# Splitting four weight tiles early in a one-core decoder-layer kernel, and loading them as ready-made parts

## The chip, the cores and the metric

The kernel runs on 1 core of one Trainium2 chip. The metric is the device time of one launch in microseconds (us), as a median of several runs; one further execution was taken by the hardware profiler, and all rows below are of that execution.

## The reference, cut to what matters

One layer of a decoder is computed for 1024 prompt positions and 64 sample positions (8 sequences of 8), model width 1024, all in float32.

```python
h = rmsnorm(x, norm_mix)
q, k, v, gu, gv, ga, gb = split_in(h @ w_in)
o = attention over a window of 128 with sinks (q, k, v)        # prompt; samples with a cache
s = spatial_gating(gelu(gu), layernorm(gelu(gv)))              # gMLP branch
merged = sigmoid(ga) * (o @ w_pa) + sigmoid(gb) * (s @ w_pb)   # w_pa: 1024 x 1024, w_pb: 768 x 1024
x = x + merged @ w_out
x = x + conv_ffn(rmsnorm(x, norm_ffn))
y = rmsnorm(x, norm_final)
```

The change concerns `w_pa`, the weight of the attention branch: eight tiles of 128 output columns each, and only how four of them reach on-chip memory.

## The kernel before, in words

**Precision.** Each float32 operand of a large matmul is split in two parts of the type that TensorE takes at its faster rate: `hi` is a rounded copy, `lo = x - hi`. A product is then three matmuls, hi·hi, hi·lo and lo·hi. The helper `split` (lines 39 to 41) makes the copy on ScalarE (ACT, line 40) and the difference on VectorE (DVE, line 41).

**Weights.** The class `Weights` streams all weight tiles in a fixed order of units. A tile is loaded raw by SyncE's DMA queue (SP) into one of four `wraw` buffers (line 146), split into one of four `wh`/`wl` slots in two halves of 128x512, and handed to the matmuls by `get()`. In its ordinary use `get()` splits one unit ahead and loads three ahead. There is also a form `add_pre`: the parts lie ready in device memory, and the unit is two DMAs straight into `wh` and `wl`, with no raw buffer and no split (line 194). Before the change only the first up-projection pairs (`upd`) go that way.

**Stages around the change.** All tokens are in two groups: group 0 has the 64 sample tokens and 512 prompt tokens (576 columns), group 1 the other 512 prompt tokens.
1. The pair phase (to about 454 us): the input projection as 17 pairs of tiles, each by a seven-product scheme (`Chain.product`, line 301). After each product `behind(at, j)` takes one job from a list: first `done` and `jobs`, then `lns` (layer norm and gMLP mixing, `mix_job`), then two steps of `prep` (the loads of `prepare_samples`). The last pairs are number 14 and 15, both over both groups (15 runs group 0's seven products, then group 1's), and number 16, over group 1 alone.
2. Attention of group 0 (about 454 to 572 us), interleaved with the matmuls of the gMLP branch (`branch`, line 241, tile `s`): eight tiles of `w_pb`.
3. The opening of group 1's attention (about 572 to 584 us): the first merge matmuls of group 0 (`merge`, tiles `oh`, `ol`), while the keys, queries and values of group 1 are loaded (lines 1005, 1008, 1020, 1023).
4. Attention of group 1 (about 584 to 667 us), interleaved with the rest of group 0's merge (eight tiles of `w_pa`), and with the first two tiles of group 1's.
5. The rest of group 1's merge, the output projection, and the feed-forward part.

So `w_pa` passes twice through on-chip memory, once for each group, and each tile is split twice.

The order of the instructions on each engine is not that of the source: a scheduler orders them by its own estimate of when they are ready. Each engine then runs its list in order, SP too: a DMA that waits on SP holds up all later ones there.

Of the kernel before, what the change touches and what calls it, by code (L numbers as in the profile page):

```python
# [6 lines left out]
F32 = mybir.dt.float32  # L7
F32R = mybir.dt.float32r
# [7 lines left out]
P = 128  # L16
D = 1024
KD = 8
# [6 lines left out]
NG = 6  # L25
# [6 lines left out]
PA0, WO0, UP0, DN0 = 40, 48, 56, 100  # L32


def layer(tc, a):
    nc = tc.nc
# [10 lines left out]
    with ExitStack() as top:  # L47
# [197 lines left out]
        W = Weights(top.enter_context(tc.tile_pool(name="wp", bufs=2)), 4, 4)  # L245
# [22 lines left out]
        def wt(i):  # L268
            return a["wt"][i].rearrange("p (k c) -> p k c", c=P)
# [65 lines left out]
        dr = lambda name, shape, dt=F32: dram.tile(shape, dt, name=name)  # L335
# [11 lines left out]
        sd_ = [[dr(f"sd{g}{c}", [P, 2, n]) for c in range(NG)] for g, n in ((0, 576), (1, 512))]  # L347
        msd = [dr(f"msd{c}", [P, 576]) for c in range(KD)]
        upd = [[dr(f"upd{f}_{j}", [P, 2, 4, P]) for j in range(7)] for f in range(NPRE)]
        mbd = [[dr(f"mbd{g}{c}", [P, n]) for c in range(KD)] for g, n in ((0, 576), (1, 512))]  # L350

        apart = ("g", KD - 1, KD - 1)
# [6 lines left out]
        with ExitStack() as ph1:  # L359
# [9 lines left out]
            def stage(n):  # L369
                return stg.tile([P, 576], F32, name="stg")[:, :n]  # L370
# [45 lines left out]
                W.add(a["wpb"][c].rearrange("p (k c) -> p k c", c=P), NG)  # L416
            for at in (PA0, PA0, WO0, WO0):
                for c in range(8):
                    W.add(wt(at + c), KD)

            order = [*range(FEW, 9), 0, *range(9, 15), 1, *range(15, NFF), 2]
            for f in range(NPRE):
# [321 lines left out]
            none = lambda: None  # L744
# [44 lines left out]
            def ln_load(n):  # L789
                if n < len(lnn):  # L790
                    if "lnp" not in late:
                        lnp = late["lnp"] = poola("ln", 1, lno)
                        for x in ("lng", "lnb"):
                            late[x] = lnp.tile([P, GW], F32, name=x)
                            nc.sync.dma_start(late[x], a[x])
                    g, i = lnn[n]
                    m = NS if groups[g]["toks"][i][0] == "s" else P
                    lnv[n] = late["lnp"].tile([P, GW], F32, name="v", bufs=4)[0:m]
                    nc.sync.dma_start(lnv[n], gvd[groups[g]["toks"][i][0]][0:m])
# [27 lines left out]
            def ln_half(n, e):  # L827
                def go():
                    if e == 0:
                        ln_load(n + 1)  # L830
                        if n:
                            ln_out(n - 1)
                    else:
                        ln_store()
                        if n < len(lnn):
                            ln_stats(n)
                return go

            lns = [lambda: ln_load(0), *(ln_half(n, e) for n in range(len(lnn) + 1) for e in range(2))]
# [27 lines left out]
            def mix_load(i):  # L867
                if i < 2 * NG:
                    g, c = i // NG, i % NG
                    gr, n = groups[g], groups[g]["n"]  # L870
                    vn = late["mp"].tile([P, 4, P], F32, name="vn", bufs=2)
                    nc.sync.dma_start(vn, vnd[g][:, c, 1 - g:5 - g])
                    gu = stage(n)
                    nc.sync.dma_start(gu, gud[c][:, gr["off"]:gr["off"] + n])
                    mixin[i] = vn, gu
# [3 lines left out]
            def mix_store():  # L879
                if mixed:  # L880
                    g, c, t = mixed.pop(0)
                    sx = late["mp"].tile([P, 2, 576], F32R, name="sx")[:, :, :groups[g]["n"]]
                    split(sx[:, 0], sx[:, 1], t)
                    nc.sync.dma_start(sd_[g][c], sx.bitcast(F32))

            def mix_job(g, c):
                def go():
                    mix_store()
                    mix_load(NG * g + c + 1)
                    gr, mp = groups[g], late["mp"]  # L890
                    n, soff, has_s = gr["n"], gr["soff"], g == 0
                    vn, gu = mixin.pop(NG * g + c)
                    t, bsc = stage(n), late["bsb"][:, c:c + 1, :]
                    if has_s:
                        V.tensor_mul(t[:, 0:NS], late["sm"][:, c], gu[:, 0:NS])
                    ps = psa.tile([P, 512], F32, name="mx", bufs=1)
                    for i in range(4):
                        PE.matmul(ps[:, P * i:P * i + P], vn[:, i], late["wst"][:, c, :],  # L898
                                  start=True, stop=True)
                    V.tensor_add(t[:, soff:n].rearrange("p (b t) -> p b t", t=P),  # L900
                                 ps.rearrange("p (b t) -> p b t", t=P), bsc.to_broadcast([P, 4, P]))
                    V.tensor_mul(t[:, soff:n], t[:, soff:n], gu[:, soff:n])
                    mixed.append((g, c, t))
                return go

            mxo = ExitStack()
            lns += [mix_first, none, none, mix_samples, lambda: mix_load(0), none] + [mix_job(g, c) for g in range(2) for c in range(NG)] + [mix_store]
            lns_of = len(lns)

            def a_finish(pair, g, zs, es, last=False):  # L910
# [118 lines left out]
                return [operands(0), values(0)]  # L1029

            done, prep = [], []

            def behind(at, j):

                if done:
                    done.pop(0)()
                if jobs:
                    jobs.pop(0)()
                elif lns and at > 5 and (j % 2 == 0 or lns_of - n_half < len(lns) < lns_of):
                    lns.pop(0)()  # L1040
                elif prep and j:
                    for go in prep[:2]:
                        go()
                    del prep[:2]

            for at, (pair, gs, whole) in enumerate(seq):
# [8 lines left out]
                if not whole:  # L1055
                    for j in range(7):
                        w = W.get(min(3, 8 - j) if at == len(seq) - 1 else 3, 4 if at == len(seq) - 1 and j > 3 else 1)
                        for ch in chains[::1 - 2 * ((7 * at + j) % 2)]:
                            ch.product(j, w)
                        behind(at, j)  # L1060
                    done += fin[0] + fin[1]
                    continue
                ws, to = [], W.used + 7
                for j in range(7):
                    ws.append(W.get(min(3, 6 - j)))
                    chains[0].product(j, ws[j])
                    behind(at, j)
# [8 lines left out]
                for j in range(7):  # L1076
                    chains[1].product(j, ws[j])
                    if gs[0] == j == 0:
                        W.load(W.units[to][0] + 3)
                    W.emit(to + j)  # L1080
                    behind(at, j)
# [373 lines left out]
            for c in range(KD):  # L1455
                for at, go in enumerate(merge(1, c, operand(1)) if c > 1 else [none, none, *first[c][2:]]):
                    if at == 1:
                        t, u = held.pop(c)
# [508 lines left out]
        tops.close()  # L1967


NSTG, FEW, NPRE = 4, 3, 2  # L1970
DN_ORDER = (5, 0, 2, 4, 6, 1, 3)
T_AT = {5: 0, 3: 1, 0: 2, 4: 3, 1: 4, 2: 5, 6: 6}
OUTS = dict(y=(KD, P, T), kp=(P, 2, P), vp=(P, 256), ksn=(P, 2, NS), vsn=(8, 8, 256),
# [83 lines left out]
```

## Time and profile before

| | |
|---|---|
| median of 3 runs | 1508.78 us (1507.86 to 1512.05) |
| the profiled execution's own time | 1506.67 us |
| its span (first to last instruction) | 1504.8 us |
| mean granted TensorE clock | 0.998 of full speed |
| busy share: PE, PEld, DVE, ACT, POOL | 99%, 98%, 77%, 55%, 19% |
| moved by DMA | 286.10 MB, mean 190 GB/s |

PE is TensorE's matmul stream, PEld its weight loads, which overlap the matmuls. A matmul's recorded duration includes its way through the array, so matmuls that follow each other closely overlap in the record, and a short gap between two of them does not show as idle PE.

### The profile page before, as it was taken

Reading aid. Unit: us, or ns where it says so; the run is one execution under the profiler, and the core shown is the slowest. Engines: PE = TensorE matmul, PEld = TensorE weight load, DVE = VectorE, ACT = ScalarE, POOL = GpSimd, SP = SyncE. Lnnn points to the kernel's source line nnn. Section 1 sums busy time; section 2 is a strip of 40 time slices with the busy share of each in tenths; the row PEclk is TensorE's granted clock in tenths of the full one; section 3 lists DMA queues with packets and bytes.
Section 4 is the critical chain, followed back from the end, with each engine's and each line's share of the span. In section 5 each row is a group of like instructions: output and inputs, shape, how many; then the busy total and the mean of one; then the engine's idle time right before and its main releaser. Section 6 shows DMA issues by size and latency. Waiting matters only on the chain.

```text
span 1504.8 us, 31429 instructions
## 1 busy us (share of the span) xinstructions
PE 1491.9 (99%) x12166; PEld 1478.9 (98%) x12166; DVE 1160.2 (77%) x1956; ACT 833.0 (55%) x1802; POOL 279.8 (19%) x438
## 2 busy tenths in 40 slices
PE   9999999999999999999999999999999999999997
PEld 9999999999999999999999999999999999999997
DVE  6877779656545996989678888898898888785675
ACT  7656764454553874864444655655555556453563
POOL 2001003101020332430223222232142122000002
PEclk9999999999999999999999999999999999999999
DMA  8552558547659757859978433332332317973454
GB/s 282 178 191 94 177 198 281 182 156 262 223 183 329 250 185 222 254 178 316 338 244 279 139 113 116 123 119 99 110 126 106 103 64 236 369 242 98 129 176 134
DMA packets 136868, 286.10 MB, mean 190 GB/s; under 512 B 15248, under 2 KB 43792, under 8 KB 136720
## 3 DMA queue, kind: packets, MB, share of 16 engines
q1 hardware_dynamic: 131904, 279.57, 55.7%
q10 hardware_dynamic: 4816, 4.54, 0.9%
q8 instruction: 95, 1.56, 0.4%
q14 instruction: 53, 0.43, 0.1%
HBM read 195.56 MB, written 90.46 MB: 190 GB/s over the span
## 4 chain that ended last, share of the span: by engine, by line
PE 91%; DVE 4%; ACT 1%; DMA 1%; issue 1%; SPq 0%; DVEq 0%; ACTq 0%
PE st L301 52%; PE dn L1796 15%; PE mm L241 14%; PE st L532 6%; PE sc L1289 1%; PE mx L898 1%; PE po L1350 1%; DVE s L1315 1%; DVE nm L1305 1%; DVE s L1299 1%; DMA wraw<-wt 1%; ACT s L1312 1%; DMA q<-qd 0%; PE pt L1322 0%; DVE wl L41 0%
## 5 line engine op out<-in xcount | busy, mean ns | idle before, releaser
L301 PE MATMUL st<-th,wh 128*128 128x256 f32 (+1 forms) x2128 | 610.4, 287 | 0.3 <-ACT k L282 0.2
L301 PE MATMUL st<-tl,wh 128*128 128x256 f32 (+1 forms) x2128 | 608.5, 286 | 0.0
L301 PE MATMUL st<-th,wl 128*128 128x256 f32 (+1 forms) x2128 | 608.1, 286 | 0.0
L301 PEld LDWEIGHTS st<-th,wh 128*128 128x128 f32 x2128 | 399.9, 188 | 1.6 <-ACT k L282 0.9
L301 PEld LDWEIGHTS st<-th,wl 128*128 128x128 f32 x2128 | 400.2, 188 | 0.0
L301 PEld LDWEIGHTS st<-tl,wh 128*128 128x128 f32 x2128 | 399.7, 188 | 0.0
L40 ACT CAST wh<-wraw 128x512 fp32r<-128x512 f32 (+1 forms) x244 | 144.1, 611 | 87.3 <-PE st L301 33.1
L41 DVE TENSOR_TENSOR wl<-wraw,wh 128x512 fp32r<-128x512 f32 (+1 forms) x244 | 165.2, 693 | 32.6 <-ACT wh L40 30.8
L1796 PE MATMUL dn<-th,wh 128*128 128x288 f32 (+1 forms) x616 | 176.7, 287 | 0.0
L1796 PE MATMUL dn<-tl,wh 128*128 128x288 f32 (+1 forms) x616 | 176.2, 286 | 0.0
L1796 PE MATMUL dn<-th,wl 128*128 128x288 f32 (+1 forms) x616 | 175.1, 284 | 0.0
L40 ACT CAST wh<-ws 128x512 fp32r<-128x512 f32 x160 | 98.1, 622 | 97.0 <-PE st L301 70.7
L41 DVE TENSOR_TENSOR wl<-ws,wh 128x512 fp32r<-128x512 f32 x160 | 109.2, 695 | 49.3 <-ACT wh L40 47.8
L1796 PEld LDWEIGHTS dn<-th,wl 128*128 128x128 f32 x616 | 115.9, 188 | 0.0
L1796 PEld LDWEIGHTS dn<-tl,wh 128*128 128x128 f32 x616 | 115.7, 188 | 0.0
L1796 PEld LDWEIGHTS dn<-th,wh 128*128 128x128 f32 x616 | 115.6, 188 | 0.0
L289 POOL TENSOR_TENSOR z<-ku,k 128x256 f32<-128x256 f32 (+1 forms) x32 | 30.9, 969 | 317.3 <-ACT ku L284 240.8
L40 ACT CAST th<-traw 128x544 fp32r<-128x544 f32 (+1 forms) x85 | 54.0, 642 | 48.4 <-PE dn L1796 36.6
L41 DVE TENSOR_TENSOR tl<-traw,th 128x544 fp32r<-128x544 f32 (+1 forms) x85 | 61.3, 728 | 21.8 <-ACT th L40 21.6
L241 PE MATMUL mm<-s,wh 128*128 128x256 f32 (+1 forms) x384 | 76.6, 294 | 0.1
L282 ACT COPY k<-st 128x256 f32<-128x256 f32 (+1 forms) x152 | 56.0, 382 | 34.8 <-PE st L301 33.9
L241 PE MATMUL mm<-oh,wh 128*128 128x256 f32 (+1 forms) x256 | 73.4, 287 | 0.1
(310 smaller groups left out, 3185.0 us busy)
## 6 DMA issues: line engine op xcount, KB each, us to landing
wraw<-wt SPq DMA_DIRECT2D x133, 512.0 KB
traw<-td SPq DMA_DIRECT2D x77, 272.0 KB
td<-za SPq DMA_DIRECT2D x22, 544.0 KB
wraw<-wt SPq DMA_DIRECT2D x35, 256.0 KB
upd<-hl SPq DMA_DIRECT2D x14, 512.0 KB
td<-t SPq DMA_DIRECT2D x11, 544.0 KB
qd<-q SPq DMA_DIRECT2D x8, 576.0 KB
q<-qd SPq DMA_DIRECT2D x8, 576.0 KB
```

The costliest lines, as they stand in the source:

```text
L40: S.copy(hi, src)
L41: V.tensor_sub(lo, src, hi.bitcast(F32))
L241: PE.matmul(ps[:, lo:lo + c1 - c0], u[:, k, :], v[:, c0:c1], start=(clear and k == 0 and i == 0), stop=(k == nk - 1 and i == 2), skip_grou ...
L282: S.copy(t, src)
L289: op(to, pick(x, to, lo, hi), pick(y, to, lo, hi))
L301: PE.matmul(ps, u[:, kk, :], v, start=first and kk + i == 0, stop=kk == 3 and i == 2, skip_group_check=True)
L532: PE.matmul(ps, u, v[:, k, :], start=k + i == 0, stop=k == KD - 1 and i == 2)
L898: PE.matmul(ps[:, P * i:P * i + P], vn[:, i], late["wst"][:, c, :], start=True, stop=True)
L1289: PE.matmul(ps[:, h, o0:256], q, kst[kv][:, e, k0:cur + P], start=e == 0, stop=e == 1)
L1299: V.copy_predicated(s[:, :, 0:P], late["mprev"].to_broadcast([P, 4, P]), ps[:, :, 0:P])
L1305: V.tensor_reduce(nm, s, AX.X, ALU.max, negate=True)
L1796: PE.matmul(place(m, e), u[:, m, :], v[:, lo:hi], start=new and i + k == 0 and (e == 0 or m % 2 == 0), stop=i == NU - 1 and k == 2, skip_g ...
```

## The change

Four of the eight tiles of `w_pa` (`NPA = 4`, tiles 0 to 3) are split once, at the end of the pair phase, in a new list of jobs `pre`, which `behind` serves after odd-numbered products once `lns` is empty (and ahead of `prep`). Each tile is done in two halves: a raw load of 256 KB, one split, and a store of both parts (512 KB) to a new memory tensor `pad`. For both groups these four tiles are then units of the form `add_pre`: two loads of 512 KB each, into `wh` and `wl`. The pool of the mixing stage is closed as a last `lns` job, to make room for `pre`'s buffers.

```diff
+        pad = [dr(f"pad{c}", [P, 2, KD, P]) for c in range(NPA)]
...
             for at in (PA0, PA0, WO0, WO0):
                 for c in range(8):
-                    W.add(wt(at + c), KD)
+                    if at == PA0 and c < NPA:
+                        W.add_pre(pad[c], KD)
+                    else:
+                        W.add(wt(at + c), KD)
...
-            lns += [mix_first, none, none, mix_samples, lambda: mix_load(0), none] + [mix_job(g, c) for g in range(2) for c in range(NG)] + [mix_store]
+            lns += [mix_first, none, none, mix_samples, lambda: mix_load(0), none] + [mix_job(g, c) for g in range(2) for c in range(NG)] + [mix_store, mxo.close]
...
+            preo, pre_in, pre_out = ExitStack(), {}, []
+
+            def pre_load(n):
+                if n < 2 * NPA:
+                    t = pre_in[n] = pre_in["p"].tile([P, 4, P], F32, name="praw")
+                    nc.sync.dma_start(t, wt(PA0 + n // 2)[:, n % 2 * 4:n % 2 * 4 + 4])
+
+            def pre_first():
+                pre_in["p"] = poola("pre", 2, preo)
+                pre_load(0)
+
+            def pre_split(n):
+                def go():
+                    pre_load(n + 1)
+                    while pre_out:
+                        nc.sync.dma_start(*pre_out.pop(0))
+                    if n < 2 * NPA:
+                        t, to = pre_in.pop(n), pre_in["p"].tile([P, 2, 4, P], F32R, name="phl")
+                        split(to[:, 0], to[:, 1], t)
+                        pre_out.append((pad[n // 2][:, :, n % 2 * 4:n % 2 * 4 + 4], to.bitcast(F32)))
+                    else:
+                        preo.close()
+                return go
+
+            pre = [pre_first, *(pre_split(n) for n in range(2 * NPA + 1))]
...
                 elif lns and at > 5 and (j % 2 == 0 or lns_of - n_half < len(lns) < lns_of):
                     lns.pop(0)()
+                elif pre and not lns and j % 2:
+                    pre.pop(0)()
                 elif prep and j:
...
-NSTG, FEW, NPRE = 4, 3, 2
+NSTG, FEW, NPRE, NPA = 4, 3, 2, 4
```

## Rows read from the trace of the kernel before

**Rows 1.** The page, part 1: busy us, share of the span, instructions.

```profile
PE 1491.9 (99%) x12166; PEld 1478.9 (98%) x12166; DVE 1160.2 (77%) x1956; ACT 833.0 (55%) x1802; POOL 279.8 (19%) x438
```

**Rows 2.** The page, part 4: the chain that ended last, by engine.

```profile
PE 91%; DVE 4%; ACT 1%; DMA 1%; issue 1%; SPq 0%; DVEq 0%; ACTq 0%
```

**Rows 3.** Windows, attention stages: length, PE, PEld, DVE, ACT, POOL busy, clock, DMA, GB/s.

```profile
535.00:556.00 21.00, 20.56 (x167) 20.04 (x165) 20.35 (x41) 16.98 (x53) 7.43 (x17) 1.00 0.48 139
556.00:578.00 22.00, 21.97 (x174) 21.32 (x173) 14.02 (x29) 9.29 (x23) 6.33 (x15) 1.00 0.51 172
578.00:620.00 42.00, 41.68 (x320) 40.13 (x319) 32.31 (x60) 27.96 (x94) 13.36 (x29) 1.00 0.92 245
620.00:667.00 47.00, 46.74 (x364) 44.71 (x363) 44.77 (x89) 37.00 (x114) 22.28 (x48) 1.00 0.62 194
```

**Rows 4.** The same windows, tile wl alone (DVE column: the differences of the splits).

```profile
535.00:556.00 21.00, 9.25 (x33) 6.05 (x32) 2.73 (x4) 0.00 (x0) 1.00 0.48 139
556.00:578.00 22.00, 13.75 (x49) 9.09 (x48) 2.58 (x4) 0.00 (x0) 1.00 0.51 172
...
620.00:667.00 47.00, 20.68 (x70) 13.10 (x70) 5.58 (x8) 0.00 (x0) 1.00 0.62 194
```

**Rows 5.** The page, part 5: one split of a raw half tile, ACT and DVE.

```profile
L40 ACT CAST wh<-wraw 128x512 fp32r<-128x512 f32 (+1 forms) x244 | 144.1, 611 | 87.3 <-PE st L301 33.1
L41 DVE TENSOR_TENSOR wl<-wraw,wh 128x512 fp32r<-128x512 f32 (+1 forms) x244 | 165.2, 693 | 32.6 <-ACT wh L40 30.8
```

**Rows 6.** Waits of PEld, 535 to 670 us: us in total, times, longest.

```profile
PEld sc L1289 <- DVE s L1299: 1.8, 9, 0.3
PEld po L1350 <- issue: 0.7, 3, 0.3
PEld po L1350 <- ACT s L1312: 0.6, 1, 0.6
```

**Rows 7.** Windows, end of the pair phase, columns as in Rows 3.

```profile
402.00:412.00 10.00, 10.00 (x83) 10.00 (x82) 3.29 (x5) 5.96 (x14) 0.00 (x0) 1.00 0.64 219
412.00:422.00 10.00, 10.00 (x84) 10.00 (x83) 5.71 (x11) 3.70 (x8) 1.72 (x2) 1.00 0.04 13
422.00:432.00 10.00, 10.00 (x80) 10.00 (x79) 1.64 (x3) 4.28 (x9) 0.00 (x0) 1.00 0.52 180
432.00:442.00 10.00, 10.00 (x85) 10.00 (x85) 4.36 (x8) 5.39 (x11) 6.99 (x19) 1.00 0.38 109
442.00:452.00 10.00, 10.00 (x91) 10.00 (x90) 5.42 (x10) 6.28 (x15) 2.04 (x4) 1.00 1.03 412
452.00:462.00 10.00, 9.94 (x112) 8.72 (x110) 3.79 (x10) 6.21 (x15) 1.16 (x3) 1.00 1.03 383
```

**Rows 8.** SP's own timeline: loads of prepare_samples, first and last of 15 from L965, L978, L947.

```profile
435.51 0.38 SPq L965 DMA_DIRECT2D kn<-ksn  x1
...
446.57 0.33 SPq L978 DMA_DIRECT2D cvc<-cv  x1
```

**Rows 9.** SP's own timeline, opening of group 1's attention: start, issue us, line.

```profile
569.11 0.37 SPq L146 DMA_DIRECT2D wraw<-wt  x1
...
574.29 0.33 SPq L146 DMA_DIRECT2D wraw<-wt  x1
575.10 0.32 SPq L1138 DMA_DIRECT2D stg<-sg0d  x1
575.47 1.18 SPq L1005 DMA_DIRECT2D kst<-kd  x2
576.74 1.01 SPq L1008 DMA_DIRECT2D q<-qd  x2
```

**Rows 10.** The chain that ended last, 566 to 586 us: start, us, what.

```profile
569.11 3.29 DMA wraw<-wt
...
576.74 7.40 DMA q<-qd
...
584.28 0.71 PE sc L1289 x4
```

**Rows 11.** Windows, first scores of group 1, columns as in Rows 3.

```profile
580.00:590.00 10.00, 9.73 (x74) 9.40 (x73) 4.20 (x7) 2.20 (x5) 0.00 (x0) 1.00 1.11 274
```

## The prediction

> **What bounds the kernel now.** I read the page first. TensorE is busy 99% by its matmuls and 98% by its weight loads (PEld) [rows 1], and the chain that ended last is PE for 91%, DVE for 4% [rows 2]. So the kernel is TensorE's work plus a few gaps, and only gaps can be won. They have to be looked for where the chain leaves PE, which is in the two attention stages. There I cut windows around the work that the change touches [rows 3]. The reader is to see two things. In 620 to 667 us DVE is busy 44.77 of 47 us, nearly full, and in 535 to 556 it is 20.35 of 21. And PE looks full in the same windows (46.74 and 20.56), while PEld shows 44.71 and 20.04, 2.29 and 0.96 us short. At the end of the pair phase PEld is 10.00 of 10 [rows 7], so a PEld that falls short is TensorE not being fed, and I take PEld's idle time as the most that can be won. The waits of PEld between 535 and 670 us [rows 6] say what for: the largest named one is the score matmuls waiting for DVE's masking, 1.8 us over 9 times; the next ones are 0.7 and 0.6. They are many small gaps, none a stall of its own.
>
> The Trainium skill says the same of the two columns ("Perfetto Trace Analysis", section "Identifying the Most-Contended Engine": matmul busy share is no good measure of headroom, the weight loads' share is); by the matmul column the two windows would leave 0.26 and 0.44 us to win, by the weight loads 2.29 and 0.96.
>
> **The change part by part.** The sum is made against the profiled execution's 1506.67 us (span 1504.8 and 1.9 around it); the median of the runs shown is 2.11 above it.
>
> *Splits taken out.* Four tiles, two groups, two halves: 16 splits of 611 ns on ACT and 693 ns on DVE [rows 5], 9.8 and 11.1 us of work. Where they lay: four halves in 535 to 556 (DVE 2.73 us), four in 556 to 578 (2.58), eight in 620 to 667 (5.58) [rows 4]; these are tiles 0 and 1, tiles 2 and 3 of group 0, and all four of group 1, because a tile is split some units before it is used. In the middle window DVE is busy 14.02 of 22 us [rows 3], so nothing is won there. In the other two DVE is nearly full, so the 2.73 and 5.58 us let DVE reach the masking and the transposed probabilities earlier. The bounds are 0 (PE's gaps there are not DVE's doing) and the PEld gaps, 0.96 + 2.29 = 3.25 us. Not all of that is waiting for DVE: part of it is the change from one shape of matmul to another, and of the named waits [rows 6] the DVE one is 1.8 us over the whole stretch. I take half of the ceiling, -1.6 us.
>
> *Splits put in.* Eight, at 611 + 693 ns: 4.9 us on ACT, 5.5 on DVE, between about 404 and 447 us. (The last pair has 84 matmuls, and 10 us hold about 84 [rows 7], so a two-group pair is some 20 us and the last one 10: pair 14 begins near 454 - 50 = 404.) What hides them: DVE is busy 1.64 to 5.71 and ACT 3.70 to 6.28 in each 10 us there, while PEld is 10.00 [rows 7]. Added, DVE has some 1.3 us more in each 10. I cost it 0. Without that cover (an ACT that waits for a late load in front of a PSUM copy), it would be one split, 1.3 us, each time.
>
> *DMAs put in.* Eight raw reads of 256 KB and eight stores of 512 KB: 6.3 MB. DMA engines are busy 0.64, 0.04, 0.52 and 0.38 in the four windows from 402 to 442 [rows 7], so about 24 of 40 us are free; at the 412 GB/s that they reach in 442 to 452 that is 9.9 MB. It fits. From 442 on they are full (1.03), and a 0.52 MB store that slips there pushes the loads of group 0's attention back by 1.3 us. SP issues 16 more DMAs there, at 0.3 to 0.5 us each as the issues of [rows 8, 9], 6 us of 40 in which it has gaps of over 10 us.
>
> *A step moved.* The 12 steps of `prep` gave way to `pre` at odd products; they now end in the last pair rather than in pair 15. In the trace before, their 15 loads issue from 435.51 to 446.57 [rows 8], behind each other, as soon as group 0's operands are let go. Behind them stand the raw loads of `w_pb` and the loads of keys and queries for group 0. Bounds: 0 (they are still issued when their memory is free, because the scheduler goes by readiness) to about three slipped stores, 3.9 us. I take 0: their memory, not their place in the list, is what they wait for.
>
> *Loads changed.* For each of the eight units one 512 KB load into a raw buffer becomes two of 512 KB into a `wh`/`wl` slot: 1.05 MB, 4.2 MB more in all. The wait changes too: a raw load waits for DVE to finish an earlier split, the new ones wait for TensorE to be done with the tile four units before. With four slots that is three tiles ahead of use; a tile's matmuls are 96 (some 12 us at 84 in 10 us) without the attention between them, and the 512 KB load took 3.29 us [rows 10]. So no matmul waits for the weights themselves. What counts is who is behind them on SP. At the opening of group 1's attention the chain runs through SP: the raw loads at 569.11 and 574.29, a gate load at 575.10 that waited for its buffer, then `kst` and `q`, and `q` took 7.40 us to land [rows 9, 10]; the first score matmuls started at 584.28, and there PEld is 0.60 short in 10 us [rows 11]. There is no slack at this place. Tiles 2 and 3 of group 0 get their slots when the last two tiles of the gMLP branch end, just before 573. Bounds: 0 (both are through before `kst` is issued, as DMA is only half busy, 0.51, in 556 to 578 [rows 3]) and both of them in front of `q`: 2.1 MB at the 274 GB/s of that window [rows 11], 7.7 us; at 412 GB/s 5.1. The nearest row is the raw load at 574.29, which stands ahead of `kst` and is half the size of one such unit; tile 2 is a few us earlier. I take a quarter of one unit at 412 GB/s, +0.6 us.
>
> The Trainium skill ("DMA: Bandwidth & Descriptors", section "Bandwidth") gives about 358 GB/s as what memory leaves one core, by which the two units would be 5.9 us; this trace moved 412 GB/s over 10 us [rows 7], so the measurement decides.
>
> *Sum:* -1.6 + 0 + 0 + 0 + 0.6 = -1.0 us, 1505.7 for a profiled execution; with the 2.11 that the median stands above it, 1507.8 us.
>
> **The rivals.**
> *DVE sets the pace (faster).* If DVE at 95% is the limit of both attention windows, what it loses is won: 2.73 + 5.58 = 8.3 us, 1500.5. For it: 44.77 of 47 us busy. Against: PEld shows only 3.25 us of gaps there, and TensorE's work does not shrink; it would need gaps outside these windows to close too (578 to 620 has 1.87 [rows 3]). Half of it, 4 us, is the likelier end.
> That is also where the Trainium skill's rule leads ("Perfetto Trace Analysis", the same section: the engine with the highest occupancy is to be optimized first); by that rule 1500.5, by the PEld gaps no less than 1505.5.
>
> *The opening is late (slower).* Both new loads stand ahead of `kst` and `q` on SP: 5.1 to 7.7 us, less the 1.6 won later: 1512.3 to 1514.9. It decides for slower when the first scores start over 6.1 us later than 584.28 on the same base. For it: the chain goes through this queue and PE waits at its end. Against: DMA is half idle before, and other merge matmuls are ready and could be put in front.
>
> *Group 0's attention is late (slower).* `prep` and the last stores meet in 442 to 462, where DMA is full and PEld falls to 8.72 of 10 [rows 7]: up to 3.9 us from the stores and 2.9 from the later `prep` loads (two products of 12 matmuls, at 84 in 10 us), less the 1.6: 1514.0. For it: no free DMA there. Against: 24 us of free DMA before it.
>
> *Nothing is won.* DVE's time is freed where PE's gaps are those of changing shapes; the load costs nothing either: 1508.8.
>
> **How the numbers follow.** A difference under 0.3% (4.5 us) is about what a measurement of this kernel cannot tell from no change: the three runs span 4.2 us. Forecast (a gain of 0 to 3 us less a small loss) 0.48; nothing won 0.20; DVE sets the pace 0.13; the opening late 0.13; group 0's attention late 0.06. Faster by over 0.3% (below 1504.3) is the DVE case and little else, 0.14. Slower (above 1513.3) is two thirds of the opening's case, most of the other, and a scheduler's order that turned out worse, 0.16. Same: 0.70. Range: from 1503.5 (two thirds of the DVE case's gain) to 1513.0 (the opening's loss at 412 GB/s and a little), which leaves out about one in five.
>
> **What would show it.** Right: 16 fewer splits of `wh<-wraw` and eight of `phl`; DVE in the 47 us window near 620 down by some 5.6 us; PEld's gaps there down by one to two; PEld still 10.00 in 402 to 442; first scores of group 1 within a microsecond or two of where they were, counted from the end of the pair phase. Wrong: `q<-qd` landing over 6 us later at the opening; the first sample scores waiting for `ckt` or `s`; stores of `phl` still going out after 447; or attention of group 1 shorter by 4 us or more.

## The result, and the profile after

| | before | after |
|---|---|---|
| median | 1508.18 us (19 runs, 1506.47 to 1512.05) | 1510.79 us (19 runs, 1507.90 to 1517.90) |
| ratio | | 1.0021, 95% interval 1.0011 to 1.0030 |
| profiled execution (span) | 1506.67 us (1504.8) | 1510.66 us (1508.9) |

The change made the kernel slower by 0.21%, some 3 us. The forecast was 1 us faster. (One execution of a later run, g1only, took 3305.5 us and is left out of its ratio.) The page's first part, the chain by engine and the splits of the kernel after, which answer to [rows 1, 2, 5]:

```profile
PE 1491.4 (99%) x12166; PEld 1479.4 (98%) x12166; DVE 1159.2 (77%) x1948; ACT 828.6 (55%) x1794; POOL 276.4 (18%) x438
...
PE 89%; DMA 4%; DVE 3%; ACT 2%; issue 1%; SPq 0%; DVEq 0%; ACTq 0%
...
L40 ACT CAST wh<-wraw 128x512 fp32r<-128x512 f32 (+1 forms) x228 | 134.7, 610 | 87.3 <-PE st L301 33.0
...
L41 DVE TENSOR_TENSOR wl<-wraw,wh 128x512 fp32r<-128x512 f32 (+1 forms) x228 | 153.6, 691 | 30.1 <-ACT wh L40 28.2
```

Sixteen raw splits are gone and TensorE's work is the same. What is new is DMA in the chain: 4% instead of 1%. TensorE now waits for transfers, directly or through another engine. The four rows of the PE timeline that begin after such a wait (the bracket is the idle time before, and what ended it):

```profile
429.17 0.40 PE L301 MATMUL st<-th,wh 128*128 128x288 f32 x1 [1.46 <-ACT k L282]
...
463.89 0.33 PE L1253 MATMUL pt<-c_ident,s 128*128 128x128 f32 x1 [1.00 <-ACT s L1240]
464.61 0.30 PE L1254 MATMUL pt<-c_ident,sx 128*64 128x128 f32 x1 [0.39 <-DVE sx L1243]
...
588.03 0.71 PE L1320 MATMUL sc<-kst,q 128*128 128x256 f32 x4 [1.68 <-DMA q<-qd]
```

Three places, then: **A** at 429 us in the last pair of the pair phase, **B** at 463 in the start of group 0's attention, **C** at 588 in the opening of group 1's. Before, C was 0.3 us and the others did not exist: together 4.3 us are lost. Against them stands the gain, in windows of the kernel after laid where the same work now is, some 3 to 4 us later than in [rows 3, 7] (columns as there):

```profile
422.00:432.00 10.00, 8.54 (x66) 8.30 (x65) 3.09 (x6) 6.38 (x13) 0.00 (x0) 1.00 0.91 298
...
538.00:559.00 21.00, 20.60 (x170) 20.26 (x169) 19.70 (x38) 15.62 (x51) 6.60 (x16) 1.00 0.66 214
559.00:581.00 22.00, 22.00 (x176) 21.86 (x176) 11.41 (x24) 6.92 (x19) 5.64 (x16) 1.00 0.52 173
...
623.75:670.75 47.00, 46.80 (x375) 45.80 (x374) 40.32 (x80) 32.87 (x104) 20.73 (x46) 1.00 0.77 243
```

PEld (the second count) gains 0.22, 0.54 and 1.09 us on [rows 3], 1.85 together, and falls to 8.30 at A, where [rows 7] had 10.00. So 4.3 - 1.85 = 2.4 us lost by the end of group 1's attention: its last product starts at 669.75, before at 667.38. The other 1.6 of the 4.0 us between the two profiled executions come later, without a wait, and 1.3 of them in the next 35 us. The three lines show the same work in the kernel before, in the kernel after, and in a second profile of the kernel after (run again, below):

```profile
680.00:690.00 10.00, 10.00 (x90) 10.00 (x90) 10.00 (x18) 3.64 (x6) 0.00 (x0) 1.00 0.91 300
```
```profile
684.00:694.00 10.00, 10.00 (x87) 10.00 (x87) 10.00 (x17) 4.19 (x7) 0.00 (x0) 1.00 0.91 297
```
```profile
688.00:698.00 10.00, 10.00 (x90) 10.00 (x90) 10.00 (x17) 4.45 (x8) 0.00 (x0) 1.00 0.92 311
```

The clock reads 1.00 and both PE columns are full in all three, yet fewer matmuls fit into the second: they start every 118 ns there and every 113 ns in the other two. The third line is the changed kernel too, so this pace belongs to the execution and not to the change.

**A, ScalarE's list.** The ACT timeline of the kernel after:

```profile
420.36 0.62 ACT L40 CAST phl<-praw 128x512 fp32r<-128x512 f32 x1 [1.33 <-DMA pad<-phl]
...
425.43 0.62 ACT L40 CAST phl<-praw 128x512 fp32r<-128x512 f32 x1 [1.11 <-DMA pad<-phl]
...
427.20 0.62 ACT L40 CAST phl<-praw 128x512 fp32r<-128x512 f32 x1
427.73 0.38 ACT L319 ACTIVATE z<-st 128x256 f32<-128x256 f32 x1
428.20 0.63 ACT L942 ACTIVATE z<-z 128x512 f32<-128x512 f32 x1
428.74 0.68 ACT L282 COPY k<-st 128x288 f32<-128x288 f32 x2
```

An early split's copy waits until the store two splits before has left its `phl` buffer (there are two). ACT runs its list in order, so all behind it waits too, at the end the copies of a product's sums (L282) that TensorE waits for.

**B, ScalarE's list again.** The ACT timeline of the kernel before, then of the kernel after, from the copy of the first sample scores on (L1202, now L1233):

```profile
456.25 0.39 ACT L1202 COPY s<-sc 128x272 f32<-128x272 f32 x1 [0.40 <-ACT z L938]
456.65 1.28 ACT L1209 ACT_TABLE_LOAD   x1
...
459.89 0.93 ACT L40 CAST wh<-wraw 128x384 fp32r<-128x384 f32 x2 [0.75 <-DMA wraw<-wpb]
```
```profile
458.19 0.39 ACT L1233 COPY s<-sc 128x272 f32<-128x272 f32 x1 [0.40 <-ACT z L942]
459.81 0.93 ACT L40 CAST wh<-wraw 128x384 fp32r<-128x384 f32 x2 [1.23 <-DMA wraw<-wpb]
461.10 0.93 ACT L40 CAST wh<-wraw 128x384 fp32r<-128x384 f32 x2 [0.36 <-DMA wraw<-wpb]
462.04 1.28 ACT L1240 ACT_TABLE_LOAD   x1
```

The last of the 15 loads of `prepare_samples` went out 9.4 us later than in [rows 8] (456.00), with two raw loads of `w_pb` now among them. But that is not what TensorE waits for: the first scores are there 1.9 us later, as all of TensorE's work is by then, and the next split of `w_pb` starts at 459.81, before at 459.89. What changed is ACT's order. Before, the table load and the exponentials of the first scores came ahead of these splits; now they stand behind them, and the splits wait for their raw loads.

**C, the opening.** SP's timeline and the chain, which answer to [rows 9, 10]:

```profile
576.06 0.42 SPq L194 DMA_DIRECT2D wh<-pad  x1
...
577.00 0.43 SPq L194 DMA_DIRECT2D wl<-pad  x1
577.47 1.36 SPq L1009 DMA_DIRECT2D kst<-kd  x2
579.25 0.98 SPq L1012 DMA_DIRECT2D q<-qd  x2
```
```profile
579.25 8.64 DMA q<-qd
588.03 0.71 PE sc L1320 x4
```

Two pad loads of 512 KB, those of tile 3, stand ahead of the keys and queries, and `q` takes 8.64 us where it took 7.40.

### The profile page after: what moved, and what is told of

Its sections match the earlier page's. It is cut to its first block, busy times and chain, and to the rows that moved or that the text cites. A ratio compares the mean times of both kernels' runs of the same rounds, so it can differ in the third digit from the quotient of the medians.

```text
span 1508.9 us, 31457 instructions
## 1 busy us (share of the span) xinstructions
PE 1491.4 (99%) x12166; PEld 1479.4 (98%) x12166; DVE 1159.2 (77%) x1948; ACT 828.6 (55%) x1794; POOL 276.4 (18%) x438
## 4 chain that ended last, share of the span: by engine, by line
PE 89%; DMA 4%; DVE 3%; ACT 2%; issue 1%; SPq 0%; DVEq 0%; ACTq 0%
PE st L301 49%; PE dn L1827 15%; PE mm L241 14%; PE st L536 6%; PE sc L1320 1%; DMA pad<-phl 1%; ACT s L1343 1%; PE mx L902 1%; DMA wraw<-wpb 1%; PE po L1381 1%; DMA q<-qd 1%; PE pt L1353 1%; DVE s L1346 1%; DVE s L1330 0%; DVE nm L1336 0%
## 5 line engine op out<-in xcount | busy, mean ns | idle before, releaser
L40 ACT CAST wh<-wraw 128x512 fp32r<-128x512 f32 (+1 forms) x228 | 134.7, 610 | 87.3 <-PE st L301 33.0
L41 DVE TENSOR_TENSOR wl<-wraw,wh 128x512 fp32r<-128x512 f32 (+1 forms) x228 | 153.6, 691 | 30.1 <-ACT wh L40 28.2
L241 PE MATMUL mm<-oh,wl 128*128 128x256 f32 (+1 forms) x256 | 73.9, 289 | 0.0
```

Source lines behind the costliest of these rows:

```text
L40: S.copy(hi, src)
L41: V.tensor_sub(lo, src, hi.bitcast(F32))
L241: PE.matmul(ps[:, lo:lo + c1 - c0], u[:, k, :], v[:, c0:c1], start=(clear and k == 0 and i == 0), stop=(k == nk - 1 and i == 2), skip_grou ...
```

## The experiments

"Ratio" is always to the kernel before, with its 95% interval. Waits are those of the profiled execution.

### B: the move alone, and the move undone

```diff
 # prep_moved: the kernel before, prep served only where the change serves it
-                elif prep and j:
+                elif prep and j and not (j % 2 and (at < len(seq) - 1 or j == 1)):
```

> The kernel before with one edit: the sample loads (prep) are put where the change puts them, three of their six slots in pair 15 and three in pair 16; no early splits, no ready parts. Theory of three waits: the move alone makes group 0's attention start late (the raw loads of the gMLP branch land behind the late sample loads, and ACT waits for them in front of the first exponentials): +1.5 us, 1510.2 where before is 1508.7, with transposes that wait near 463. Rival, the move costs only because the early stores have filled the queue: within 0.5 us of before. Rival, the scheduler issues these loads by readiness, wherever they stand: same.

Ratio 1.0014 [1.0002, 1.0026]. The PE timeline has the wait near 463 and nothing near 429:

```profile
462.39 0.33 PE L1222 MATMUL pt<-c_ident,s 128*128 128x128 f32 x1 [0.88 <-ACT s L1209]
463.11 0.30 PE L1223 MATMUL pt<-c_ident,sx 128*64 128x128 f32 x1 [0.39 <-DVE sx L1212]
```

No transfer was added here: the steps' place in the list alone brings B and costs 2 us. Nor is a load late that ACT waits for: the two raw loads of `w_pb` were issued from 449.62 us on, before from 450.78. ACT's list has their splits (458.49 and 459.60) ahead of the table load (460.54) here too, as in every profile with B. Why the scheduler orders it so when the steps are moved is not shown.

```diff
 # every: the changed kernel, a step after every product
-                elif pre and not lns and j % 2:
+                elif pre and not lns:
```

> The changed kernel with one edit: the early splits take a step after every product, not only after odd ones, so that they are over before the sample loads (prep) are due, and prep keeps its old places. Theory of three waits (early splits held up by their own stores and in front of PSUM copies on ACT, 1.5 us near 425; prep late and with it the start of group 0's attention, 1.4 us near 463; keys and queries of group 1 behind two new loads, 1.4 us near 585; less 1.9 us won in the attention stages): the second wait goes, so about 1.4 us less than the changed kernel, 1509.4 where before is 1508.2; the first scores' transposes near 463 don't wait. Rival, the added memory traffic costs: no change from the changed kernel, 1510.8. Rival, only the schedule came out unlucky: anything within 1.5 us of 1510.8, with other waits.

Ratio 0.9998 [0.9989, 1.0007]. With `pre` done sooner, `prep` is back early, ACT's table load (458.26) is again ahead of the splits of `w_pb` (461.27), and B is gone. A is down to 0.76 us, C is 1.91. One condition less takes back the whole loss. All transfers of the change are still made, so their bytes alone are not the price.

### A: the stage alone, its buffers, its engine

```diff
 # early_unused: the changed kernel, both groups load w_pa raw as before
-                    if at == PA0 and c < NPA:
+                    if False:
```

> The changed kernel with one edit: the parts are split and stored early as in the change, but nobody loads them; both groups load and split the four tiles as before. Theory of three waits: the wait near 429 (ACT held by the early splits, +1.7) and the one near 463 (prep late, +1.5) stay, the one at the opening of group 1's attention and all that was won go: 1511.9 where before is 1508.7. Rival, the loads into the slots are what costs: 1508.7. Rival, the added traffic costs in proportion (6.3 of 10.5 MB): 1510.3.

Ratio 1.0034 [1.0021, 1.0047]: A (0.73 us in this execution) and B (1.12 and 0.39), no gain, no C. The stage and the move cost this before anything is loaded.

```diff
 # phl3: a third buffer for the split parts
-... pre_in["p"].tile([P, 2, 4, P], F32R, name="phl")
+... pre_in["p"].tile([P, 2, 4, P], F32R, name="phl", bufs=3)
```

> The changed kernel with one edit: three buffers instead of two for the early split's parts. Theory of three waits: the early splits don't wait for the store of two splits before, ACT's PSUM copies are on time, TensorE's 1.5 us wait near 429 goes; about 1509.3 where before is 1508.2. Rival, the added memory traffic costs: 1510.8, the same traffic. Rival, ACT is late there for the split's own 0.6 us and not for the store: the wait stays.

Ratio 1.0022 [1.0008, 1.0036], and A stays, 1.22 us. The waits of 418 to 432 us say why:

```profile
ACT phl L40 <- DMA praw<-wt: 3.0, 3, 1.7
```

The copies no longer wait for the store but for the raw load. That the store alone makes A is wrong; another transfer that the copy waits for does it too.

```diff
 # dve_copy: the changed kernel, the copy on DVE
-                        split(to[:, 0], to[:, 1], t)
+                        V.tensor_copy(to[:, 0], t)
+                        V.tensor_sub(to[:, 1], t, to[:, 0].bitcast(F32))
```

> The changed kernel, in which the rounded copy of the eight early splits is made on DVE in place of ACT, nothing else. Theory (the wait near 429 us comes from the early splits' copies in ACT's list, which wait for a transfer and hold up the copies of the product's sums behind them): that wait falls from 1.46 us to under 0.4, the waits near 463 and at the opening stay, and the time is about 1.5 us under the changed kernel's: ratio to before 1.0009 to 1.0014. Rival (the transfers themselves or DVE's work are what delays the product): the wait stays above 1 us, ratio 1.002 or more.

Ratio 1.0006 [0.9994, 1.0017]. No wait near 429 is left, while DVE's copies wait for the same stores:

```profile
DVE phl L1054 <- DMA pad<-phl: 2.5, 1, 2.5
```

B (1.00 and 0.39) and C (1.96) are as they were. So A comes through ScalarE's list, not from the transfers by themselves: DVE stood as long and nothing that TensorE needed was behind it. This run takes the copies' own 0.6 us off ACT together with their waits, so it does not part the two; in the list of the kernel after both stand ahead of L282 (1.11 us of wait, then two copies).

### C: which loads, and which group

```diff
 # g1only: the changed kernel, group 0 loads raw
-            for at in (PA0, PA0, WO0, WO0):
+            for n, at in enumerate((PA0, PA0, WO0, WO0)):
...
-                    if at == PA0 and c < NPA:
+                    if n == 1 and c < NPA:
```

> The changed kernel with one edit: only group 1 loads the ready parts, group 0 loads and splits its four tiles as before the change. Theory of three waits: keys and queries of group 1 land as before (first scores' wait back from 1.7 to 0.3 us), the small gain of group 0's own tiles (some 0.5 us) goes: about 1.0 us less than the changed kernel, 1509.8. Rival, the added memory traffic costs (4.2 of 10.5 MB go): also about 1.0 less, but with the 1.7 us wait still there or gone elsewhere. Rival, DVE's relief is what decides: with half the splits back, slower than the changed kernel, 1511.5 or more.

Ratio 1.0015 [1.0004, 1.0027]. C is down to 0.31 us. A was 3.64 us and B 1.69 and 0.39 in the profiled execution, the slowest of the eleven that count; the ratio cannot be told from the change's 1.0021.

```diff
 # rawload: the kernel before; four tiles of both groups as two loads, of stored queries
+                    if at == PA0 and c < 4:
+                        x = qd[0][c].rearrange("p e n -> p (e n)")[:, 0:KD * P]
+                        W.add_pre(x.rearrange("p (k c) -> p k c", c=P), KD)
```

> The kernel before, with the four tiles of both groups loaded by two loads straight into their slots from other parts that lie in memory (so their values are not the weight's; the early splits and stores are left out altogether). That is the change without its price in the pair phase. Theory of three waits: the wait near 429 and the one near 463 go, the one near 585 stays (+1.4), 1.9 us are won in the attention stages: 1507.7 where before is 1508.2. Rival, the added memory traffic costs: 4.2 of 10.5 MB remain, 1509.2. Rival, DVE sets the pace: with 11 us of it gone and nothing put in, 1503 or less.

Ratio 0.9998 [0.9987, 1.0009]. No A, no B, and C at 1.90 us. The loads alone make C. The next three divide them; the values of the tiles concerned are not the weight's in these either.

```diff
 # raw_01 / raw_23 / raw_g1: as rawload, with this condition
+                    if n == 0 and c in (0, 1):    # raw_01
+                    if n == 0 and c in (2, 3):    # raw_23
+                    if n == 1 and c < 4:          # raw_g1
```

> The kernel before, in which group 0's pass alone takes its tiles 0 and 1 as two loads of 512 KB each without a split, from memory that holds the queries' parts (these two tiles' values are not the weight's). Theory (the late opening is the pad loads of tiles 2 and 3 on the queue ahead of the keys and queries): the first scores of group 1 wait under 0.5 us for q, and group 0's attention ends 0.8 us earlier; ratio 0.9993 to 0.9998. Rival (the opening is paced by its transfers, so that any earlier end of group 0's attention is taken back there): the first scores wait 0.9 us or more for q, with no pad load ahead of it; ratio 0.9998 to 1.0003.

> The same with tiles 2 and 3 of group 0 in place of 0 and 1, and these alone. Theory (pad loads ahead of the keys and queries): the first scores wait 1.2 us or more for q, which takes 8.5 us or more to land; ratio 1.0005 to 1.0010. Rival (what counts is an earlier end of group 0's attention): they wait as before, under 0.5 us; ratio 0.9998 to 1.0003.

> The kernel before, in which group 1's pass alone takes its four tiles as two loads of 512 KB each without a split; they come from memory that holds the queries' parts, so these four tiles' values are not the weight's. No early stage, and prep where it was. Theory (the gain of the splits taken out is real and shows once nothing in front of it is late): no wait near 429 or 463, the opening as before (the first scores wait under 0.5 us), PEld in the 47 us of group 1's attention 1 to 2 us fuller, ratio 0.9988 to 0.9993. Rival (what is won in group 1's attention is given back behind it, or was the other group's): ratio 0.9997 to 1.0005.

raw_01: 0.9987 [0.9976, 0.9997]; raw_23: 1.0014 [1.0002, 1.0025]; raw_g1: 0.9989 [0.9977, 1.0001]. In raw_01 and raw_g1 the first scores do not wait for `q`; in raw_23 they do:

```profile
585.52 0.71 PE L1293 MATMUL sc<-kst,q 128*128 128x256 f32 x4 [1.37 <-DMA q<-qd]
```
```profile
576.52 8.86 DMA q<-qd
```

So the loads of tiles 2 and 3 cost 2 us, and those of tiles 0 and 1 win as much; for raw_g1 the interval does not exclude that nothing is won. Of the win of raw_01, 0.79 us are seen in its PEld in two windows of [rows 3]:

```profile
535.00:556.00 21.00, 20.63 (x167) 20.28 (x167) 19.66 (x40) 15.83 (x55) 6.63 (x16) 1.00 0.64 198
556.00:578.00 22.00, 22.00 (x178) 21.87 (x177) 12.70 (x27) 8.15 (x19) 5.98 (x14) 1.00 0.53 170
```

```diff
 # own_queue: every, and group 1's first keys and queries issued by ACT
+                def kq(kv):
+                    return nc.scalar if g == 1 and kv == 0 else nc.sync
...
-                                nc.sync.dma_start(q.bitcast(F32), qd[g][c])
+                                kq(kv).dma_start(q.bitcast(F32), qd[g][c])
```

> The kernel that takes an early step after every product, in which the first keys and queries of group 1 (four DMAs) are issued by ACT instead of SP, so that they no longer stand behind a gate load and the pad loads on SP; nothing else. Theory (the opening's wait is the order on SP's queue): they are issued 3 to 4 us earlier against the end of group 0's attention, the first scores wait under 0.5 us (1.7 to 2.3 before), ratio 0.9984 to 0.9992. Rival (the transfers share the same DMA engines, so that an earlier issue brings no earlier landing, or ACT itself is held up by the four issues): the first scores still wait over 1 us, ratio 0.9996 to 1.0005.

Ratio 1.0075 [1.0047, 1.0103]: a miss of both theories. The issues on ACT waited themselves, and ACT stood behind them (its timeline, in the slowest execution of the six):

```profile
583.61 7.12 ACTq L1015 DMA_DIRECT2D q<-qd  x2
590.82 1.14 ACT L40 CAST wh<-wraw 128x512 fp32r<-128x512 f32 x2 [11.33 <-DMA dvst<-dvd]
```

The queries were issued later and not earlier, and the first scores waited 5.07 and 1.85 us for them. So the run does not test whether an earlier issue would mend C; it shows ACT's list held up for 11.33 us. The Trainium skill ("DMA: Bandwidth & Descriptors", section "Issuing engines are not separate DMA queues") has it that issuing from another engine saves no more than issue time. This run agrees that nothing is saved, and shows what it can cost.

### Together

```diff
 # every_g0two: every, and group 0 takes pads for tiles 0 and 1 alone
+                    if at == PA0 and c < (2, NPA)[n]:
 # all_mended: every_g0two, and the copies of the early splits on DVE, as in dve_copy
```

> The kernel 'every' (early splits after every product, prep in its old places) with one more edit: in group 0 only tiles 0 and 1 are loaded as parts, 2 and 3 are loaded raw and split as before; group 1 loads all four as parts. Theory of three waits: the wait of the first scores of group 1 goes back from some 1.5 to 0.3 us, what was won in the attention stages stays (those two tiles lay in a stretch in which DVE had room), the wait near 429 (0.8) stays: some 1.2 us below 'every', 1507.5 where before is 1508.7. Rival, the opening is late for another reason (order of the queue): first scores as late as in 'every' and the time too.

> The kernel 'every_g0two' with one more edit: in the early splits DVE makes the rounded copy too, so that ACT, which copies the pair phase's products out of PSUM, has nothing to do with them. Theory of three waits: no wait near 429, none near 463, none at the opening, about 1.9 us won in the attention stages: 1506.8 where before is 1508.7, the only version that is faster than before. Rival, the waits move to DVE (its own sums of the pair phase stand behind the splits, which wait for the same DMAs): a wait of TensorE for DVE near 429 and 1507.8 or more. Rival, nothing can be won, as TensorE's gaps are changes of shape: 1508.7.

1.0004 [0.9993, 1.0015] and 1.0005 [0.9994, 1.0016]. all_mended has neither A nor B, yet the first scores wait 1.52 us for `q` in it and 1.20 in every_g0two, with no pad load ahead. Both expectations were missed there, and raw_01, which has the same loads for group 0, shows no such wait. From the first issue of `kst` to the first scores it is 9.8 us in all_mended and 9.4 in every_g0two, 8.8 before and about 8.2 in raw_01, with the same DMAs in the same order on SP.

```diff
 # store_parts: the kernel before; group 0's pass stores its slots, group 1's loads them
+                        if g == 0 and c in KEPT and e == 1 and k0 == 0:
+                            for i, x in enumerate(st["w"]):
+                                nc.sync.dma_start(pad[c][:, i], x.bitcast(F32))
...
+                    if n == 1 and c in KEPT:
+                        W.add_pre(pad[c], KD)
...
+KEPT = (0, 1, 2, 3)
```

> The kernel before, in which group 0's pass splits its four tiles as before and stores both parts from their slots to memory, and group 1's pass loads them as parts. No early stage, and prep where it was: 16 loads and eight splits less than the change puts in. Theory: no wait near 429 or 463, the opening as before or some 0.5 us later (two stores of 512 KB for each tile stand on the queue in group 1's attention, behind the opening), group 1's last tiles a few us less of DVE: ratio 0.9990 to 0.9996. Rival (the stores meet the loads of keys, queries and sums, and a wait on a transfer takes the gain's place): ratio 1.0003 to 1.0015, with waits on kst, q or stg in group 1's attention.

Median 1506.86 us (1508.10 for the kernel before beside it), ratio 0.9986 [0.9974, 0.9999]: faster than both kernels, by an interval that ends just under 1. Its first scores start at 584.26, as before (584.28), so the window of [rows 3] can be set beside it line for line:

```profile
620.00:667.00 47.00, 46.82 (x376) 45.76 (x376) 40.46 (x82) 33.47 (x105) 21.02 (x47) 1.00 0.82 269
```

DVE loses 4.31 us, PEld gains 1.05. The splits saved are those of group 1 alone; the parts that the first pass makes anyway are kept, with no early stage, no moved step and no pad load at the opening. The profiled execution as a whole does not show the gain (1506.74 us, before 1506.67): from about 668 to 703 us its matmuls ran at the slower of the two paces shown above, 87 of them in 680 to 690 against 90, which took back 1.3 us.

> The kernel store_parts with all eight tiles kept: group 0's pass stores both parts of each, and group 1's pass splits none. The last tiles of group 1 come after its attention, where DVE was busy 10.51 of 13 us and PEld 12.69. If the gain of store_parts is DVE's time in group 1's attention alone, it stays at a ratio of 0.9984 to 0.9990; if the eight more stores of 512 KB meet the loads of group 1's attention, 0.9995 to 1.0010.

With `KEPT = tuple(range(8))` the ratio is 1.0055 [1.0042, 1.0068]. The last tiles come where DMA was 0.86 to 0.92 busy already (667 to 720 us of the kernel before), and now a load is late, and the clock falls behind the wait (PE timeline, then windows):

```profile
686.24 0.36 PE L241 MATMUL mm<-oh,wh 128*128 128x256 f32 x1 [4.29 <-DMA wh<-pad]
```
```profile
682.00:692.00 10.00, 5.06 (x23) 4.88 (x24) 7.07 (x11) 2.58 (x4) 0.00 (x0) 0.74 1.03 407
692.00:702.00 10.00, 10.00 (x84) 10.00 (x83) 4.19 (x6) 1.30 (x2) 0.00 (x0) 0.92 1.04 412
```

### The change once more

> The changed kernel unchanged, for a second profile: if the three waits are the schedule's and not one execution's, all three stand in it again (near 429, 463 and 588 us, each within 1 us of 1.5, 1.7 and 1.7).

1514.30 us. All three waits stand in it, but C was 3.00 us, not within 1 of 1.7, and behind B and C the granted clock fell:

```profile
464.00:468.00 4.00, 2.91 (x26) 2.30 (x27) 2.82 (x8) 2.85 (x12) 0.31 (x2) 0.80 1.03 421
468.00:472.00 4.00, 4.00 (x35) 3.58 (x35) 1.02 (x6) 1.27 (x5) 0.00 (x0) 0.77 1.04 350
...
592.00:596.00 4.00, 4.00 (x24) 4.00 (x23) 0.71 (x1) 0.58 (x1) 0.00 (x0) 0.59 1.19 258
```

So the places of the waits belong to the schedule, and their price to the execution.

## Why the prediction was wrong, by its steps

The range held the time, the sign did not.

**Splits taken out, -1.6: the right way and near in size.** PEld gained 1.85 us in the kernel after. By the ratios it is 2.0 us for group 0's tiles 0 and 1 (raw_01) and 1.7 for group 1's four (raw_g1), with 1.6 and 1.8 us to either side, so that their sum cannot be told from 1.85. Of the 1.85 us, 0.54 came from 559 to 581, where the prediction expected nothing. That DVE sets the pace fell: in store_parts DVE lost 4.31 us of a window in which it was 95% busy, and TensorE won 1.05. The Trainium skill's rule to optimize the engine of highest occupancy first ("Perfetto Trace Analysis", section "Identifying the Most-Contended Engine") hardly chooses there, with DVE at 44.77 us and PEld at 44.71; by the measurement PEld's gaps were the measure, as the same section says of TensorE.

**A step moved, 0: the first step that failed.** "Their memory, not their place in the list, is what they wait for" is wrong: with a later place in the list, and no transfer added, the last of them went out at 453.94 instead of 446.57, and that run has B and cost 0.14% (prep_moved). Yet B is not the lateness of these loads. With the steps moved, the scheduler set the splits of `w_pb` ahead of the first exponentials on ACT, and the prediction had no term for that; a worse order stands in it only as a part of the chance of slower. The price lay inside its bounds of 0 to 3.9 us, which were worked out from slipped stores, so that is luck. Group 0's attention late, given 0.06, was the rival that named the place, and full DMA was not what made it.

**Splits put in, 0: the second.** The cover was read from the right rows, PEld 10.00 [rows 7], but that row says that TensorE is fed, not by how much. The step named its own failure, an ACT that waits for a transfer in front of a PSUM copy, and had the store in its list: A is that, at 1.46 us. That this is near the 1.3 of one split is luck, as A was 0.73 to 3.64 us over the profiles that have it. Both loads and stores in the added stage can make it (phl3), and ACT's list is what passes it on (dve_copy).

**Loads changed, +0.6: the right step, mis-sized.** C is 1.4 us of new wait in the kernel after, and the loads of tiles 2 and 3 cost 0.14%, 2 us, by themselves (raw_23). The step saw that there was no slack and named the two units; it took a quarter of one. `q` landed 1.24 us later after its issue, half of the 2.55 us that one unit of 1.05 MB is at the 412 GB/s of [rows 7]. The rival of the late opening had the right mechanism, and a price (5.1 to 7.7 us) some four to five times too high.

**DMAs put in, 0: not by themselves.** The last store of parts was issued at 429.9 us, 12 us ahead of the place where DMA is full. Their cost came through A.

The parts added give +0.24%: the early stage with the move cost 0.34%, tiles 2 and 3 at the opening 0.14%, against 0.13% and 0.11% won. The change measured +0.21%. That agrees, but weakly: each part has an interval of 0.1% or a little more to either side, and the sum one of 0.24%. Open is the opening in every_g0two and all_mended: 1.2 and 1.5 us of wait with nothing more ahead of `q` than before. So the loads of tiles 2 and 3 bring C (every profile that has them shows 1.37 us or more), but they are not all that can make this wait. By the same sum all_mended, with A, B and the pad loads gone, should have been 0.2% faster than before, and was not.

## What to carry to other kernels

Beside an engine that is full for a thousand microseconds, a moved instruction or a new one costs what waits behind it, not what it lasts: for each list that runs in order, ask which instruction of the critical engine's supply now stands behind a transfer. A count of busy time shows that there is room, not that there is slack; where the chain already passes through a queue with a wait of 0.3 us, a load put ahead of it is paid. A moved step can also change the order of work that it has nothing to do with, so compare the lists of all engines, not only the moved part. And work that is done twice was better saved here by keeping what the first pass makes (0.14%) than by a stage of its own, as far as the transfers behind it had room.

## What the runs showed of the hardware that was not expected

A wait of TensorE can cost twice. In the second profile of the changed kernel the granted clock was 0.80 and 0.77 in the eight microseconds from 464, where TensorE had just waited 0.97 and 0.39 us, and 0.59 in the four from 592, after a wait of 3.00: part of these stretches ran at 1.2 GHz instead of 2.4, together (0.20 + 0.23 + 0.41) x 4 = 3.4 us of full speed. In the first profile, after waits of 1.00, 0.39 and 1.68 us, it stayed at 1.00. The Trainium skill ("TensorE: Matmul & The Clock Gate", Part 1) says that a monitor sets the clock by how busy the engine was of late, and these falls do stand behind waits. The length of a wait alone does not tell: after 1.90 us in rawload and 1.96 in dve_copy the clock stood at 0.57 and 0.59 over four microseconds, after 1.91 in every it stayed at 1.00. The falls go some way with the spread of the change's runs: the five of 19 above 1515 us had a mean granted clock of 0.994 to 0.997, the profiled one 0.998. But two runs at 0.996 took 1510.34 and 1511.28 us, and a clock lower by 0.002 over the whole is 3 us of the 6, so the spread is not explained by it alone.

A stretch of matmuls can also run at two paces at a granted clock of 1.00, with both PE columns full: one started every 113 ns or every 118 ns in the lines at 680 to 698 us above, the last two of which are of the same kernel. Over 35 us that made 1.3 us, where the change cost some 3. So a full PE column does not show that two executions do the same work in the same time, and differences of 1 us between two single profiles are read from waits and not from their ends. What sets the pace is not shown.
